# A two-layer decoder trunk in split float32: the high and low weight halves move to other start addresses in SBUF

## The chip, the cores and the metric

The kernel runs on one core of a Trainium2 chip. The metric is the device time of one execution in microseconds (us); lower is better. Before the change the median of 3 runs was 2752.81 us (2752.61 to 2753.01).

## What is computed

Two decoder layers over 256 positions of width 2048, all in float32. Layer 0 mixes tokens with a Mamba-2 block, layer 1 with attention that has a forgetting gate; each layer then has a SwiGLU feed-forward block and a gated per-layer input. Cut to what matters here:

```python
for i in range(2):
    hn = rmsnorm(h, norm_mix_pre[i])
    mix = ssd_mixer(hn, ...) if i == 0 else fox_mixer(hn, ...)   # each: u @ w_in, the mixer, @ w_out
    h = h + rmsnorm(mix, norm_mix_post[i])
    hn = rmsnorm(h, norm_ffn_pre[i])
    ff = (silu(hn @ w_gate[i]) * (hn @ w_up[i])) @ w_down[i]     # 2048 -> 5632 -> 2048
    h = h + rmsnorm(ff, norm_ffn_post[i])
    pe = rmsnorm(p[i] @ ple_w_proj[i], ple_norm[i])
    h = h + sigmoid(h @ ple_w_gate[i]) * pe
```

Nearly all of the work is products of a 256-row activation with large weight matrices, some 500 MB of weights, each used once.

## The kernel before, in words

**Split products.** A float32 product is made of three products in the faster `float32r` type. An activation `x` is held as a high half (rounded) and a low half (the rest), side by side in one tile of 2 x 256 columns; a weight tile `raw` becomes a high half `wh` and a low half `wl` in the same way. The product is `wh*xh + wh*xl + wl*xh`; the term `wl*xl` is left out.

**Stages.** The weights come in 1020 stages of at most 1024 columns on 128 partitions (`emit_stage`, L160). For each, SyncE's queue issues the DMA of `raw` (L170), ScalarE rounds it to `wh` (L182), VectorE subtracts to make `wl` (L187). There are 6 buffers of `raw` and 4 each of `wh` and `wl`.

**Matmuls.** `unit` (L202) takes the stages in order. In the common form a block of 128 x 128 weights is the stationary operand and the activation is the moving one. Each block of `wh` is loaded and 512 columns (high and low activation halves) are streamed past it; then the block of `wl` at the same place is loaded and the 256 columns of the high half are streamed:

```python
PE.matmul(accs[t], lhsT=wh[:, c, t * P:(t + 1) * P],
          rhs=x.rearrange("p a n -> p (a n)"), start=st, stop=False)      # L249
last = PE.matmul(accs[t][:, :T], lhsT=wl[:, c, t * P:(t + 1) * P],
          rhs=x[:, 0, :], start=False, stop=sp)                            # L251
```

So while L249 streams its 512 columns, the weights of the following L251 are loaded, and while L251 streams its 256 columns the `wh` block of the next pair is loaded. This text calls an L249 with its L251 a pair, and the time from the start of one matmul to the start of the next a slot. The last units before a norm use a separate form (L244, L245, L246): three matmuls of 256 columns, `wh` twice, then `wl`. A third form (L238 to L240, in layer 1's value projection) has the weights as the moving operand, 412 or 416 columns wide. The products of the per-layer input (L436, L439, L440) are again three of 256 columns, with the activation tile `psp`.

**The activations** lie in several pools: `x` tiles in `xp` (the most used: normed input of the mixers and of the feed-forward block), `xq` (half of the Mamba block's output), `a` in `act0` and `act1` (the feed-forward block's hidden activations), `xb` (the input of layer 1's mixer), and `psp` at the far end.

**Where tiles lie in SBUF** is set by pools that are laid one behind another in the order in which they are opened: `cp`, `wp` (raw, wh, wl), `hp` (the residual stream `h`), `xp`, `ev` (temporaries), `gap`, and then the pools that come and go (`xq`, `xb`, `act0`, ...). Two pads of 96 bytes are there already: 24 spare columns behind the last tile of `hp` (L376), which push `xp` along, and the tile of 24 columns in `gap` (L381), which pushes all behind it. Every step inside `wh`, `wl` and the activation tiles that a matmul of the pair or of the separate form makes is a multiple of 512 bytes, so each kind of tile has one start address modulo 256 bytes for all its blocks.

The order of the instructions on each engine comes from a scheduler that does not look at addresses.

Of the kernel before, what the change touches and what calls it, by code (L numbers as in the profile page):

```python
# [7 lines left out]
F32 = mybir.dt.float32  # L8
F32R = mybir.dt.float32r
# [5 lines left out]
P = 128  # L15
# [12 lines left out]
SW = 1024  # L28
# [3 lines left out]
WB = 4  # L32
# [7 lines left out]
HELD = 6  # L40
WARM = 10
TAIL_WIDE = 2

_VEC = {}
_NV = 0
# [11 lines left out]
def tile_trunk(ctx, tc, a, out):  # L57
    nc = tc.nc
    mult, add, sub, mx_, mn_ = ALU.mult, ALU.add, ALU.subtract, ALU.max, ALU.min
    V, A, G, PE = nc.vector, nc.scalar, nc.gpsimd, nc.tensor  # L60

    def pool(stack, name, bufs=1, **kw):
        return stack.enter_context(tc.tile_pool(name=name, bufs=bufs, **kw))

    cp = pool(ctx, "cp")
    wp = pool(ctx, "wp")
    hp = pool(ctx, "hp")
    xp = pool(ctx, "xp", bufs=16)
    ev = pool(ctx, "ev", bufs=2)
    gap = pool(ctx, "gap")  # L70
# [5 lines left out]
    def nm(s):  # L76
        cnt[0] += 1
        return f"{s}_{cnt[0]}"
# [78 lines left out]
    def after(ins):  # L157
        return nullcontext() if ins is None else tc.issue_after(ins.ins)

    def emit_stage(a_ins=None, v_ins=None):  # L160
        i = len(emitted)
        cols, r, kc, n = stages[i]

        def view(t):
            return t[:, :kc * n].rearrange("p (c n) -> p c n", n=n)

        raw = wp.tile([P, SW], F32, tag="raw", name=f"raw{i}", bufs=RAWB)
        o = 0
        for W, c0, w in cols:
            nc.sync.dma_start(  # L170
                out=view(raw)[:, :, o:o + w],
                in_=W[r:r + kc * P, c0:c0 + w].rearrange("(c p) n -> p c n", p=P))
            o += w
        wh = wp.tile([P, SW], F32R, tag="wh", name=f"wh{i}", bufs=WB)
        wl = wp.tile([P, SW], F32R, tag="wl", name=f"wl{i}", bufs=WB)
        if a_ins is None:
            a_ins, turn_a[0] = turn_a[0], None
        with ExitStack() as order:
            for ins in [a_ins] + lag[0]:
                order.enter_context(after(ins))  # L180
            lag[:] = [lag[1], []]
            low_a[0] = A.copy(out=wh[:, :kc * n], in_=raw[:, :kc * n])  # L182
        with ExitStack() as order:
            for ins in [v_ins] + turn:
                order.enter_context(after(ins))
            turn.clear()
            low[0] = V.tensor_tensor(out=wl[:, :kc * n], in0=raw[:, :kc * n],  # L187
                                     in1=wh.bitcast(F32)[:, :kc * n], op=sub)
        emitted.append((view(wh), view(wl), kc))

    def next_stage(look=LOOK):
        i = taken[0]
        taken[0] += 1
        while len(emitted) < len(stages) and len(emitted) <= i + look:
            emit_stage()
        return emitted[i]
# [5 lines left out]
    def unit(rhs, evac, tok=False, pre=None, pops=1, late=(), merge=1, look=LOOK, sep=False):  # L202
# [4 lines left out]
        if nt == 6:  # L207
            merge = TAIL_WIDE
        accs = [psa.tile([P, 512], F32, tag="acc", name=nm("acc")) for _ in range(nt)]
# [168 lines left out]
    warm = cp.tile([P, 2], F32, name="warm")  # L378
    V.memset(ones, 1.0)
    V.memset(mhalf, -0.5)  # L380
    G.memset(gap.tile([P, 24], F32, name="gap0"), 0.0)  # L381
    A.activation(warm, mhalf, AF.Exp)

    def load_x(c):
# [6 lines left out]
    for c in range(3):  # L391
        emit_stage(None, None if c else lo0)
        load_x(c + 1)
# [55 lines left out]
    def post_norm(fill):  # L449
        for f in fill[:FILL_A]:  # L450
            f()
        rs = rstd_small(ssb, D)
        for _ in range(PRE_A):
            emit_stage(mark[0], dmark[0])
        for f in fill[FILL_A:FILL_B]:
            f()
        ps = rstd_wide(rs, None)
        for f in fill[FILL_B:]:
            f()
        return ps  # L460
# [976 lines left out]
```

## Time and profile before

| | |
|---|---|
| median of 3 runs | 2752.81 us |
| span of the profiled execution | 2751.0 us, 1.8 us under that median |
| TensorE (PE) busy | 2743.8 us, 100% |
| VectorE (DVE) busy | 1906.4 us, 69% |
| ScalarE (ACT) busy | 1479.8 us, 54% |
| GpSimd (POOL) busy | 48.5 us, 2% |
| DMA | 519.58 MB, mean 189 GB/s |

How to read it: PE is the row of the matmuls and PEld that of the weight loads that go on beside them. Matmuls are pipelined: one starts before the one ahead of it has left, and the end shown is modelled, so neither the busy share nor the mean duration says how fast they follow each other. That is read from the start times of the timeline. A group's row gives busy time, then the mean length of one, then the idle time of the engine just before its instructions and what ended it.

### The profile page before, as it was taken

How to read it: one execution, taken by the hardware profiler on the slowest of the kernel's cores; microseconds unless marked ns; L12 is line 12 of the kernel's file. 1: busy time of each engine (PE TensorE's matmuls, PEld its weight loads, DVE VectorE, ACT ScalarE, POOL GpSimd, SP SyncE). 2: the span in 40 equal slices, each digit the busy share in tenths (PEclk: the TensorE clock that was granted, in tenths of full speed). 3: DMA queues.
4: the chain of work that ended last, by engine and by line, in shares of the span. 5: the costliest groups of instructions: out<-in, count | busy, mean ns of one | idle time of the engine just before them, and what ended most of it. 6: DMA issues, size and time to landing. Idle time of an engine off the chain costs nothing.

```text
span 2751.0 us, 43135 instructions
## 1 busy us (share of the span) xinstructions
PE 2743.8 (100%) x16342; PEld 2434.7 (89%) x16342; DVE 1906.4 (69%) x3147; ACT 1479.8 (54%) x2455; POOL 48.5 (2%) x104
## 2 busy tenths in 40 slices
PE   9999999999999999999999999999999999999999
PEld 8888888889888888888898998889888888888898
DVE  8888888754976545666568656766876545666577
ACT  6577677554654444445456544555654444445454
POOL 0000000000000000000000000000000000000000
PEclk9999999999999999999999999999999999999999
DMA  7666666565666556666556676555666556656554
GB/s 262 187 200 192 188 193 188 163 210 166 191 201 189 190 191 189 188 175 200 195 161 196 186 221 181 177 162 163 195 206 189 187 192 188 194 169 201 198 163 167
DMA packets 262656, 519.58 MB, mean 189 GB/s; under 512 B 17408, under 2 KB 44192, under 8 KB 262448
## 3 DMA queue, kind: packets, MB, share of 16 engines
q1 hardware_dynamic: 258784, 504.54, 59.6%
q0 software_dynamic: 3520, 12.15, 1.4%
q8 instruction: 128, 2.10, 0.3%
q14 instruction: 80, 0.66, 0.1%
q10 hardware_dynamic: 144, 0.14, 0.0%
HBM read 514.58 MB, written 2.18 MB: 188 GB/s over the span
## 4 chain that ended last, share of the span: by engine, by line
PE 99%; DVE 1%; ACT 0%; issue 0%; DMA 0%; DVEq 0%; ACTq 0%
PE acc L249 58%; PE acc L251 30%; PE acc L245 1%; PE acc L246 1%; PE acc L244 1%; PE acc L238 1%; PE acc L239 1%; PE acc L240 1%; PE mi L1004 1%; PE mi L1269 0%; PE mi L1317 0%; PE mi L347 0%; PE mi L963 0%; PE acc L436 0%; PE mi L331 0%
## 5 line engine op out<-in xcount | busy, mean ns | idle before, releaser
L249 PE MATMUL acc<-x,wh 128*128 128x512 f32 x4992 | 1696.7, 393 | 0.9 <-DVE x L389 0.5
L187 DVE TENSOR_TENSOR wl<-raw,wh 128x1024 fp32r<-128x1024 f32 (+4 forms) x1020 | 1169.3, 1152 | 725.1 <-ACT wh L182 723.5
L182 ACT CAST wh<-raw 128x1024 fp32r<-128x1024 f32 (+4 forms) x1020 | 1004.2, 991 | 968.2 <-PE acc L249 841.1
L251 PE MATMUL acc<-x,wl 128*128 128x256 f32 x4992 | 1317.0, 280 | 0.1
L249 PEld LDWEIGHTS acc<-x,wh 128*128 128x128 f32 x4992 | 922.4, 188 | 189.6 <-issue 1.3
L251 PEld LDWEIGHTS acc<-x,wl 128*128 128x128 f32 x4992 | 923.6, 188 | 25.6 <-issue 2.4
L249 PE MATMUL acc<-a,wh 128*128 128x512 f32 x1232 | 425.5, 391 | 0.0
L251 PE MATMUL acc<-a,wl 128*128 128x256 f32 x1232 | 341.9, 282 | 0.0
L249 PEld LDWEIGHTS acc<-a,wh 128*128 128x128 f32 x1232 | 229.9, 188 | 47.1
L251 PEld LDWEIGHTS acc<-a,wl 128*128 128x128 f32 x1232 | 232.6, 189 | 2.2
L249 PE MATMUL acc<-xb,wh 128*128 128x512 f32 x512 | 179.4, 393 | 0.0
L277 ACT COPY tb<-acc 128x256 f32<-128x256 f32 x400 | 140.1, 369 | 49.1 <-PE acc L251 25.0
L251 PE MATMUL acc<-xb,wl 128*128 128x256 f32 x512 | 144.9, 284 | 0.0
L249 PEld LDWEIGHTS acc<-xb,wh 128*128 128x128 f32 x512 | 95.6, 188 | 19.5
L251 PEld LDWEIGHTS acc<-xb,wl 128*128 128x128 f32 x512 | 96.7, 189 | 0.8 <-issue 0.2
L249 PE MATMUL acc<-xq,wh 128*128 128x512 f32 x224 | 77.7, 390 | 0.0
L900 DVE SCALAR_TENSOR_TENSOR g<-xr,vec,g 128x256 f32<-128x256 f32 x144 | 63.4, 478 | 10.8 <-ACT g L897 10.6
L278 DVE TENSOR_TENSOR g<-acc,tb 128x256 f32<-128x256 f32 x171 | 65.1, 417 | 0.4
L251 PE MATMUL acc<-xq,wl 128*128 128x256 f32 x224 | 63.0, 282 | 0.0
L984 ACT ACTIVATE E<-ab,bias 128x128 f32<-128x128 f32 x192 | 59.9, 392 | 1.2 <-DMA ab<-acd 1.2
L301 DVE TENSOR_TENSOR ssb<-ssb,sq 128x256 f32<-128x256 f32 x120 | 50.5, 421 | 12.3 <-ACT sq L300 8.9
L337 POOL TENSOR_TENSOR rs<-ms,mhalf 128x2 f32<-128x2 f32 x18 | 22.6, 1253 | 1993.1 <-DVE ms L334 1993.1
(228 smaller groups left out, 2156.9 us busy)
## 6 DMA issues: line engine op xcount, KB each, us to landing
raw<-down SPq DMA_DIRECT2D x176, 512.0 KB, 4.1
raw<-ssd_in SPq DMA_DIRECT2D x144, 512.0 KB, 4.5
raw<-gate SPq DMA_DIRECT2D x128, 512.0 KB, 4.3
raw<-up SPq DMA_DIRECT2D x128, 512.0 KB, 4.4
raw<-fox_in SPq DMA_DIRECT2D x64, 512.0 KB, 4.2
raw<-gate SPq DMA_DIRECT2D x64, 384.0 KB, 3.3
raw<-up SPq DMA_DIRECT2D x64, 384.0 KB, 3.6
raw<-ssd_out SPq DMA_DIRECT2D x40, 512.0 KB, 3.8
```

Source lines behind the costliest of these rows:

```text
L182: low_a[0] = A.copy(out=wh[:, :kc * n], in_=raw[:, :kc * n])
L187: low[0] = V.tensor_tensor(out=wl[:, :kc * n], in0=raw[:, :kc * n], in1=wh.bitcast(F32)[:, :kc * n], op=sub)
L238: PE.matmul(o, lhsT=xh, rhs=wh[:, c, :], start=st, stop=False)
L239: PE.matmul(o, lhsT=xh, rhs=wl[:, c, :], start=False, stop=False)
L240: last = PE.matmul(o, lhsT=x[:, 1, t * P:(t + 1) * P], rhs=wh[:, c, :], start=False, stop=sp)
L249: PE.matmul(accs[t], lhsT=wh[:, c, t * P:(t + 1) * P], rhs=x.rearrange("p a n -> p (a n)"), start=st, stop=False)
L251: last = PE.matmul(accs[t][:, :T], lhsT=wl[:, c, t * P:(t + 1) * P], rhs=x[:, 0, :], start=False, stop=sp)
L277: i = A.copy(out=tb[:np_], in_=acc[:np_, T:2 * T])
L278: took[0] = (i, V.tensor_tensor(out=o, in0=acc[:np_, :T], in1=tb[:np_], op=add))
L301: last_v[0] = V.tensor_tensor(out=acc, in0=acc, in1=sq, op=add)
L900: V.scalar_tensor_tensor(out=c, in0=xr[:, k:k + T], scalar=col(f"conv_w{k}", cc), in1=c, op0=mult, op1=add)
L984: A.activation(E[:, i, b * P:(b + 1) * P], ab[:, i, lo:lo + P], AF.Relu, scale=-1.0, bias=bias3[:, b, h0 + i:h0 + i + 1])
```

## The change

The tiles `wh` and `wl` leave the pool `wp` and get pools of their own, with a pad of 64 bytes between them. The pool of `x` gets a pad of 96 bytes ahead of it, and the pad ahead of the come-and-go pools grows from 96 to 224 bytes. Sizes, counts of buffers and all arithmetic stay as they are.

```diff
+GAP_L = 16
+GAP_X = 24
+GAP_A = 56
...
     wp = pool(ctx, "wp")
+    whp = pool(ctx, "whp")
+    gap_l = pool(ctx, "gap_l")
+    wlp = pool(ctx, "wlp")
     hp = pool(ctx, "hp")
+    gap_x = pool(ctx, "gap_x")
     xp = pool(ctx, "xp", bufs=16)
...
-        wh = wp.tile([P, SW], F32R, tag="wh", name=f"wh{i}", bufs=WB)
-        wl = wp.tile([P, SW], F32R, tag="wl", name=f"wl{i}", bufs=WB)
+        wh = whp.tile([P, SW], F32R, tag="wh", name=f"wh{i}", bufs=WB)
+        wl = wlp.tile([P, SW], F32R, tag="wl", name=f"wl{i}", bufs=WB)
...
-    G.memset(gap.tile([P, 24], F32, name="gap0"), 0.0)
+    for g_, n_ in ((gap_l, GAP_L), (gap_x, GAP_X), (gap, GAP_A)):
+        G.memset(g_.tile([P, n_], F32, name=nm("gap")), 0.0)
```

What it does to the addresses, from the built programs (byte address of the first tile in a partition, and in brackets that address modulo 256):

| tile | before | after |
|---|---|---|
| `raw` | 19488 (32) | 19488 (32) |
| `wh` | 44064 (32) | 44064 (32) |
| `wl` | 60448 (32) | 60512 (96) |
| `h` | 76832 (32) | 76896 (96) |
| `x` | 93376 (192) | 93536 (96) |
| `xq`, `xb`, `a` | 137792 (64) | 138080 (96) |
| `psp` | 225248 (224) | 225248 (224) |

The distance from the moving activation to the weights that are loaded beside it, modulo 256 bytes, follows from it:

| activation | to `wh` before | to `wl` before | to `wh` after | to `wl` after |
|---|---|---|---|---|
| `x` | 96 | 96 | 192 | 0 |
| `xq`, `xb`, `a` | 224 | 224 | 192 | 0 |
| `psp` | 64 | 64 | 64 | 128 |

The instructions of PE, DVE, ACT and SP stand in the same order in both programs. The one engine whose list differs is GpSimd's, at the program's start. Before:

```order
5 L1433 UNCONDITIONAL_BRANCH
6 L381 MEMSET gap_103 128x24
7 L893 MEMSET xr_617 128x3
8 L893 MEMSET xr_631 128x3
9 L337 ISA
```

And after, at the same place:

```order
5 L1441 UNCONDITIONAL_BRANCH
6 L389 MEMSET gap_115 128x16
7 L389 MEMSET gap_117 128x24
8 L389 MEMSET gap_119 128x56
9 L901 MEMSET xr_633 128x3
10 L901 MEMSET xr_647 128x3
11 L344 ISA
```

One fill of a pad has become three; nothing else moved.

## The prediction

> **What bounds the kernel now.** I read the page first (its span, the busy row, the clock row, the chain that ended last), then the groups of instructions by shape, then the timeline at a few places. From the page:
>
> ```profile
> span 2751.0 us, 43135 instructions
> PE 2743.8 (100%) x16342; PEld 2434.7 (89%) x16342; DVE 1906.4 (69%) x3147; ACT 1479.8 (54%) x2455; POOL 48.5 (2%) x104
> PEclk9999999999999999999999999999999999999999
> PE 99%; DVE 1%; ACT 0%; issue 0%; DMA 0%; DVEq 0%; ACTq 0%
> ```
>
> The chain of waits is TensorE nearly from end to end, at the full granted clock. So only what makes its matmuls follow each other faster or slower moves the end. The groups tell how many there are:
>
> ```profile
> L249 PE MATMUL acc<-x,wh 128*128 128x512 f32 x4992 | 1696.7, 393 | 0.9 <-DVE x L389 0.5 <-DVE gz L278 0.2
> L249 PE MATMUL acc<-a,wh 128*128 128x512 f32 x1232 | 425.5, 391 | 0.0
> L249 PE MATMUL acc<-xb,wh 128*128 128x512 f32 x512 | 179.4, 393 | 0.0
> L249 PE MATMUL acc<-xq,wh 128*128 128x512 f32 x224 | 77.7, 390 | 0.0
> L244 PE MATMUL acc<-a,wh 128*128 128x256 f32 x176 | 49.0, 279 | 0.0
> L244 PE MATMUL acc<-x,wh 128*128 128x256 f32 x128 | 35.7, 280 | 0.0
> L244 PE MATMUL acc<-xq,wh 128*128 128x256 f32 x32 | 8.9, 279 | 0.0
> L239 PE MATMUL acc<-wl,xb 128*128 128x412 f32 x128 | 44.7, 350 | 0.0
> ```
>
> That is 4992 + 1232 + 512 + 224 = 6960 pairs of L249 and L251, and 336 triples of L244 to L246, 1008 matmuls of 256 columns. Idle time is nil, so a stall, if there is one, sits inside the slots. The mean lengths (393, 391) overlap and don't help; the start times do. First the `x` pairs (activation 96 bytes before the weights), then the `a` pairs (224 bytes), each with the first and the last row of a steady stretch:
>
> ```profile
> 2083.11 0.39 PE L249 MATMUL acc<-x,wh 128*128 128x512 f32 x1
> ...
> 2092.12 0.39 PE L249 MATMUL acc<-x,wh 128*128 128x512 f32 x1
> ```
>
> ```profile
> 1002.04 0.39 PE L249 MATMUL acc<-a,wh 128*128 128x512 f32 x1
> 1002.27 0.28 PE L251 MATMUL acc<-a,wl 128*128 128x256 f32 x1
> ...
> 1011.75 0.39 PE L249 MATMUL acc<-a,wh 128*128 128x512 f32 x1
> ```
>
> 26 pairs in 9.01 us are 346.5 ns a pair, 28 in 9.71 us are 346.8: the same at both distances. Over these rows L249's slot is 229 ns on the mean and L251's 118. So the pairs take 6960 x 346.7 ns = 2413 us, 88% of the span, and a change of 1 ns in a pair is 7 us.
>
> Does a slot depend on addresses at all? Matmuls of one shape, 256 columns past 128 x 128 weights, show it. Separate form, `x` (distance 96) in one place and in another, then `a` (224), then the per-layer products with `psp` (64) at two places:
>
> ```profile
> 659.95 0.28 PE L244 MATMUL acc<-x,wh 128*128 128x256 f32 x1
> ...
> 661.03 0.28 PE L244 MATMUL acc<-x,wh 128*128 128x256 f32 x1
> ```
>
> ```profile
> 1511.33 0.28 PE L244 MATMUL acc<-x,wh 128*128 128x256 f32 x1
> ...
> 1512.03 0.28 PE L244 MATMUL acc<-x,wh 128*128 128x256 f32 x1
> ```
>
> ```profile
> 1399.96 0.28 PE L244 MATMUL acc<-a,wh 128*128 128x256 f32 x1
> ...
> 1401.01 0.28 PE L244 MATMUL acc<-a,wh 128*128 128x256 f32 x1
> ```
>
> ```profile
> 683.29 0.28 PE L440 MATMUL acc<-psp,wl 128*128 128x256 f32 x1
> ...
> 684.35 0.28 PE L440 MATMUL acc<-psp,wl 128*128 128x256 f32 x1
> ...
> 686.24 0.28 PE L440 MATMUL acc<-psp,wl 128*128 128x256 f32 x1
> ...
> 686.92 0.28 PE L440 MATMUL acc<-psp,wl 128*128 128x256 f32 x1
> ```
>
> 9 slots in 1.08 us are 120 ns; 6 in 0.70 are 116.7; 9 in 1.05 are 116.7; 9 in 1.06 are 117.8; 6 in 0.68 are 113.3. So one shape has slots from 113 to 120 ns, nobody waits for data, and a stretch keeps its rate: once in step, the two reads (activation and next weights) stay in step. Two rates occur at one distance too (120 and 116.7 at 96; 117.8 and 113.3 at 64), so the distance selects among rates and does not fix one.
>
> **The change part by part.** *Addresses of the pair form.* It removes no instruction from TensorE and adds none. L249 now loads `wl` at distance 0, L251 loads `wh` at 192, for all 6960 pairs. No row of before has either distance. For the 118 ns slot of L251 the bounds are the 256-column rows: 113.3 below, 120 above. Distance 192 lies half a cycle from 64, and the two distances that the pairs have now, half a cycle apart as well, give one rate; so the `psp` rows at 64 are the nearest. They show 113.3 and 117.8; I take their middle, 115.5, a gain of 2.5 ns. For the 229 ns slot of L249 the lower bound is twice the fastest 256 columns, 226.7; the upper bound comes from the first unit, where five L249 follow each other and then five L251:
>
> ```profile
> 19.67 1.33 PE L249 MATMUL acc<-x,wh 128*128 128x512 f32 x5
> 20.83 0.75 PE L251 MATMUL acc<-x,wl 128*128 128x256 f32 x5
> 21.42 1.33 PE L249 MATMUL acc<-x,wh 128*128 128x512 f32 x5
> ```
>
> Five in 1.16 us are 232 ns; the five L251 take 0.59 us, 118 each. L249 is thus within 2.3 ns of its lower bound and I take no change for it. Together: 6960 x -2.5 ns = -17.4 us, with bounds of 6960 x (-2.3 - 4.7) = -49 us and 6960 x (3 + 2) = +35 us.
>
> *The separate form.* Two of three slots load `wh` (192), one loads `wl` (0): 672 x (115.5 - 117) ns = -1.0 us; bounds 1008 x (113.3 - 117) = -4 and 1008 x (120 - 117) = +3 us.
>
> *The value projection* (L238 to L240, 480 matmuls) has the roles exchanged and other distances; at 3 ns either way, the spread between rates of the rows above, it is 1.4 us, taken as 0.
>
> *Pads.* Two more fills on GpSimd:
>
> ```profile
> 0.74 0.12 POOL L381 MEMSET gap<- 128x24 f32 x1 [0.29 <-POOLq L1428]
> 0.79 0.13 POOL L893 MEMSET xr<- 128x3 f32 x2
> ```
>
> 0.05 us from one fill to the next, at 0.7 us, on an engine that is 2% busy; the next thing on its list is needed by a convolution that comes far later. Nothing.
>
> *What covers the other engines.* ScalarE, VectorE and the DMA write and read at shifted addresses too. A slower conversion would be hidden as long as VectorE keeps its slack, least in the first 480 us:
>
> ```profile
> 0.00:480.00 480.00, 478.47 (x2895) 413.90 (x2896) 412.58 (x735) 333.75 (x640) 23.10 (x77) 1.00 0.64 202
> L187 DVE TENSOR_TENSOR wl<-raw,wh 128x1024 fp32r<-128x1024 f32 (+4 forms) x1020 | 1169.3, 1152 | 725.1 <-ACT wh L182 723.5
> ```
>
> VectorE is busy 412.58 of 480 us there (the fourth of the columns: PE, PEld, DVE after the length), so a TensorE that needs 1% less, 475 us, still finds its weights. If L187 took 10% longer, that would be 117 us against 725 us of idle time ahead of it. Taken as 0.
>
> Sum against the profiled execution: 2751.0 - 17.4 - 1.0 = 2732.6 us; the median of the runs lies 1.8 us over that span, so **2734 us**.
>
> **The rivals.** *No change.* The reads don't meet, or the streams fall into the old step again: then the pair stays at 346.7 ns and the time at 2753 us. For it speaks that distances 96 and 224 give the same pair to 0.3 ns; against it, that one shape runs at 113 and at 120 ns. The Trainium skill (TensorE: Matmul & The Clock Gate, Part 2, the step on LDWEIGHTS) says the same as this rival: TensorE has two independent read ports, so that loading the next weights takes nothing from the running matmul. By that rule alone the change is worth 0; the spread of slots does not agree with it.
>
> *Slower: a level start.* The load and the matmul beside it begin together:
>
> ```profile
> 2083.11 0.39 PE L249 MATMUL acc<-x,wh 128*128 128x512 f32 x1
> 2083.11 0.19 PEld L251 LDWEIGHTS acc<-x,wl 128*128 128x128 f32 x1
> ```
>
> At distance 0 both reads then start at the same place of the 256-byte cycle, in every one of 6960 pairs. If that collides, L249 goes to the 232 ns of the first unit and L251, pushed out of step, to 120: 352 ns, +5.3 x 6960 = +37 us, with +3 for the separate form: 2793 us. It decides from a pair of 347.5 ns on. Against it: a collision at the start only could also be the one that puts the streams out of each other's way for the rest.
>
> *Both slots gain.* If L249 goes to 226.7 and all slots of 256 columns to 113.3, the pair is 340 ns: -46.6 us and -4 us, 2702 us. Rows show the second half of this, none the first. A sentence apart: the same page of the Trainium skill (Back-to-back issue gap) has columns / 2.4 + 2.5 ns, an estimate of 216 + 109 = 325 ns for a pair and by that of about 2600 us if every excess were the placement's; no row comes near it.
>
> **How the numbers follow.** Forecast (L251 gains 1 to 4.7 ns, L249 holds): 0.42, 2718 to 2746 us. Both gain: 0.15. No change: 0.15. Slower: 0.28, since nothing shown excludes the level start. The median of a few runs tells about 0.2% (5.5 us, 0.8 ns a pair) from no change. So faster 0.57, same 0.15, slower 0.28. The range takes in the forecast, no change, and the prices of the other two: 2696 to 2794 us; beyond lie a stronger form of either, some 0.15 together.
>
> **What would show it.** Right: start to start, L249 stays at 228 to 230 ns and L251 falls to 113 to 117, alike for `x`, `a`, `xq`, `xb`; L244 to L246 follow. Wrong: L249 at 232 or more (level start), a pair at 346 to 347 (no change), or L249 below 226 (it was not at its bound). A gain in slots that isn't in the span would show as idle time ahead of L249, released by VectorE or ScalarE.

## The result, and the profile after

The changed kernel takes 2720.88 us (median of 4 runs, 2719.67 to 2721.03) against 2752.82 us before: a ratio of 0.9882 (95% interval 0.9868 to 0.9896), 32 us faster. From the page of the changed kernel:

```profile
span 2719.0 us, 43137 instructions
PE 2711.1 (100%) x16342; PEld 2410.5 (89%) x16342; DVE 1905.3 (70%) x3147; ACT 1480.7 (54%) x2455; POOL 48.8 (2%) x106
PEclk9999999999999999999999999999999999999999
PE 97%; DVE 1%; ACT 1%; issue 1%; DMA 0%; DVEq 0%; ACTq 0%
L194 DVE TENSOR_TENSOR wl<-raw,wh 128x1024 fp32r<-128x1024 f32 (+4 forms) x1020 | 1169.4, 1152 | 694.0 <-ACT wh L189 688.9
```

TensorE's busy time fell by 32.7 us with the same count of matmuls at the same clock; VectorE's subtraction (now L194) takes what it took, 1152 ns, and only the idle time ahead of it shrank, from 725.1 to 694.0 us. So what changed is the rate of the matmuls, and little else. The timeline of the changed kernel in the steady `x` stretch, first and last row (L256 is the old L249, L258 the old L251):

```profile
2099.76 0.39 PE L256 MATMUL acc<-x,wh 128*128 128x512 f32 x1
2099.99 0.28 PE L258 MATMUL acc<-x,wl 128*128 128x256 f32 x1
...
2108.94 0.39 PE L256 MATMUL acc<-x,wh 128*128 128x512 f32 x1
```

27 pairs in 9.18 us are 340.0 ns, against 346.5 before. That is the rate of the rival "both slots gain": over all pairs of the trace at 339 to 341 ns the two slots are 226.7 and 113.3 on the mean. But it is not the rate everywhere. At 348 us, four small matmuls of a norm come between the pairs:

```profile
348.33 0.50 PE L338 MATMUL mi<-ones,gss 128*128 128x1 f32 x4
...
349.12 0.40 PE L256 MATMUL acc<-x,wh 128*128 128x512 f32 x1
...
353.32 0.40 PE L256 MATMUL acc<-x,wh 128*128 128x512 f32 x1
353.56 0.22 PE L354 MATMUL mi<-identr,rh 128*128 128x128 f32 x1
...
354.46 0.39 PE L256 MATMUL acc<-x,wh 128*128 128x512 f32 x1
354.80 0.39 PE L256 MATMUL acc<-x,wh 128*128 128x512 f32 x1
...
356.84 0.39 PE L256 MATMUL acc<-x,wh 128*128 128x512 f32 x1
```

Behind them 12 pairs take 4.20 us, 350 ns each, without a wait; then other small matmuls come (L354), and behind those 7 pairs take 2.38 us, 340 ns each. Same tiles, same placement, two rates, and the change from one to the other at an interruption. This text calls such a rate a lock. Where 16 or more pairs follow each other without another matmul or a stall between them (98 stretches before, 97 after, up to 118 pairs long), none changes its rate behind its fifth pair; in the run with the distances (64, 0) further down, three of 100 do.

Added up over the whole trace from start to start (stalls, slots over 245, 130 or 200 ns, apart):

| form | count | before, mean slot | after, mean slot | us |
|---|---|---|---|---|
| 512 columns, `wh` | 6920 | 229.61 | 227.70 | -13.2 |
| 256 columns, `wl` | 6910 | 117.70 | 114.37 | -23.0 |
| separate form | 1007 | 117.18 | 117.79 | +0.6 |
| value projection | 478 | 187.29 | 189.16 | +0.9 |
| per-layer products | 184 | 116.1 | 118.4 | +0.4 |
| stalls inside these | | 10.7 us | 13.3 us | +2.6 |

The sum, -31.7 us, is the difference of the spans, 2751.0 - 2719.0, but for 0.3. Of the 5991 pairs that stand directly between two other matmuls of the pair form, 90.3% took 345 to 348 ns before; after, 85.3% take 339 to 341, 7.3% 349 to 352 and 3.7% still 345 to 348.

### The profile page after: what moved, and what is told of

It reads as the page before. It is cut to its first block, busy times and chain, and to the rows that moved or that the text cites. A ratio compares the mean times of both kernels' runs of the same rounds, so it can differ in the third digit from the quotient of the medians.

```text
span 2719.0 us, 43137 instructions
## 1 busy us (share of the span) xinstructions
PE 2711.1 (100%) x16342; PEld 2410.5 (89%) x16342; DVE 1905.3 (70%) x3147; ACT 1480.7 (54%) x2455; POOL 48.8 (2%) x106
## 4 chain that ended last, share of the span: by engine, by line
PE 97%; DVE 1%; ACT 1%; issue 1%; DMA 0%; DVEq 0%; ACTq 0%
PE acc L256 56%; PE acc L258 29%; PE acc L253 1%; PE acc L252 1%; PE acc L251 1%; PE acc L247 1%; PE acc L246 1%; PE acc L245 1%; PE mi L1012 1%; DVE wl L194 1%; ACT E L992 1%; PE mi L1277 0%; PE mi L1325 0%; ACT wh L189 0%; PE acc L444 0%
## 5 line engine op out<-in xcount | busy, mean ns | idle before, releaser
L256 PE MATMUL acc<-x,wh 128*128 128x512 f32 x4992 | 1673.4, 391 | 0.9 <-DVE gz L285 0.8
L194 DVE TENSOR_TENSOR wl<-raw,wh 128x1024 fp32r<-128x1024 f32 (+4 forms) x1020 | 1169.4, 1152 | 694.0 <-ACT wh L189 688.9
L258 PE MATMUL acc<-x,wl 128*128 128x256 f32 x4992 | 1305.2, 278 | 0.9 <-DVE wl L194 0.7
L256 PEld LDWEIGHTS acc<-x,wh 128*128 128x128 f32 x4992 | 921.8, 188 | 181.8 <-issue 1.3
L258 PEld LDWEIGHTS acc<-x,wl 128*128 128x128 f32 x4992 | 923.0, 188 | 26.4 <-DVE wl L194 3.4
L256 PE MATMUL acc<-a,wh 128*128 128x512 f32 x1232 | 417.5, 389 | 0.0
L258 PE MATMUL acc<-a,wl 128*128 128x256 f32 x1232 | 335.2, 276 | 0.0
L256 PEld LDWEIGHTS acc<-a,wh 128*128 128x128 f32 x1232 | 229.8, 188 | 46.2
L258 PEld LDWEIGHTS acc<-a,wl 128*128 128x128 f32 x1232 | 231.3, 188 | 2.1
L256 PE MATMUL acc<-xb,wh 128*128 128x512 f32 x512 | 176.6, 392 | 0.0
L258 PE MATMUL acc<-xb,wl 128*128 128x256 f32 x512 | 142.4, 279 | 0.0
L256 PEld LDWEIGHTS acc<-xb,wh 128*128 128x128 f32 x512 | 95.6, 188 | 19.2
L258 PEld LDWEIGHTS acc<-xb,wl 128*128 128x128 f32 x512 | 96.2, 188 | 0.8 <-issue 0.2
L256 PE MATMUL acc<-xq,wh 128*128 128x512 f32 x224 | 76.3, 389 | 0.0
L258 PE MATMUL acc<-xq,wl 128*128 128x256 f32 x224 | 61.7, 276 | 0.0
```

The lines of the kernel that those rows point to most:

```text
L256: PE.matmul(accs[t], lhsT=wh[:, c, t * P:(t + 1) * P], rhs=x.rearrange("p a n -> p (a n)"), start=st, stop=False)
```

## The experiments

**Theory 1** is the prediction's: each slot follows the distance of the weights that are loaded in it, L249's that of `wl`, L251's that of `wh`. **Theory 2**: activation stream and weight loads fall in step over a whole pair; a placement (both distances together) only offers locks, and what goes ahead picks one. In the runs at (96, 0), (192, 96), (64, 128) and (64, 0) only the pad sizes differ from the changed kernel, and an empty pad is not filled; distances are given as (`wh`, `wl`), so before is (96, 96) and (224, 224), after (192, 0).

### One distance at a time

`wl` level, `wh` as before, (96, 0):

```diff
-GAP_L = 16
+GAP_L = 40
```

> Weights' distances from the activation: wh 96 as before the change, wl 0 as after it. Theory 1 (each slot follows the distance of the weights loaded in it): the 512-column slot falls from 229 to 227 ns, the 256-column slot stays at 118; 6960 x -1.9 ns = -13 us, 2740 us. Theory 2 (the two loads of a pair lock together, and half of the change is not half of the gain): the pair stays near 347 ns, 2750 to 2756 us, or goes to a third rate that neither kernel shows.

`wh` as after, `wl` as before, (192, 96):

```diff
-GAP_L = 16
-GAP_X = 24
+GAP_L = 40
+GAP_X = 0
```

> Distances: wh 192 as after the change, wl 96 as before it. Theory 1: the 256-column slot falls from 118 to 114.4 ns, the 512-column slot stays at 229 to 230; 6960 x -3.3 ns = -23 us, 2730 us. Theory 2: the pair stays near 347 ns or goes to a rate of its own; 2750 us or more.

The first took 2757.09 us, a ratio of 1.0015 (1.0005 to 1.0024) to before; the second 2764.87 us, 1.0043 (1.0026 to 1.0060). Timeline of the first, then of the second, in a steady `x` stretch:

```profile
2059.85 0.39 PE L256 MATMUL acc<-x,wh 128*128 128x512 f32 x1
...
2068.86 0.39 PE L256 MATMUL acc<-x,wh 128*128 128x512 f32 x1
```

```profile
2069.71 0.40 PE L256 MATMUL acc<-x,wh 128*128 128x512 f32 x1
...
2074.94 0.40 PE L256 MATMUL acc<-x,wh 128*128 128x512 f32 x1
```

26 pairs in 9.01 us, 346.5 ns; 15 in 5.23, 348.7 ns. With `wl` level alone the 512-column slot did not fall to 227, it rose (mean 231.16) while the 256-column slot fell (116.53); with `wh` at 192 alone the 256-column slot stayed at 117.08, and the 512-column slot rose to 231.86. Either half by itself loses, 4 and 12 us, together they gain 32 us. Theory 1 falls. (The first time lies 1 us over the range that theory 2 had been given.)

### Is the cycle 128 bytes or 256?

Both distances moved by 128, (64, 128):

```diff
-GAP_X = 24
+GAP_X = 56
```

> Both distances of the changed kernel shifted by half a cycle: wh 64, wl 128. If the cycle that matters is 128 bytes, as the equal pairs at 96 and 224 before the change let one think, this is the changed kernel again: pair 340 ns, 2721 us within 5. If the cycle is 256 bytes, the pair is another one, anywhere from 340 to 352 ns, 2720 to 2795 us; more than 5 us away from 2721 decides for 256.

It took 2784.96 us, 1.0116 (1.0101 to 1.0131). Timeline:

```profile
2059.71 0.39 PE L256 MATMUL acc<-x,wh 128*128 128x512 f32 x1
...
2068.90 0.39 PE L256 MATMUL acc<-x,wh 128*128 128x512 f32 x1
```

26 pairs in 9.19 us are 353.5 ns, over the 352 that had been allowed, and a lock that neither kernel showed as its steady rate; 77% of the pairs run at 353 to 357. The half cycle of the prediction's nearest-row argument is refuted: 128 bytes make 64 us here. That 256 bytes are a whole cycle is shown for `wl` by the run of the separate form's edit, further down: its `wl` tiles are 4352 bytes long, so neighbouring buffers lie 17 x 256 bytes apart, and 84.7% of its pairs run at 339 to 341 all the same.

### A map of the placements

The changed kernel with a block of extra matmuls ahead of the first unit. They use a tile `mb` of activation values and write a PSUM tile that is not read; the column at which the weights start sets the distance:

```diff
...
+        def mm_(n, o_, m=P):
+            ins = PE.matmul(wps[:m, :n], lhsT=mb[:, o_:o_ + m], rhs=xf[:, :n], start=True, stop=True)
+            tc.keep_in_program_order(ins)
+        for rep, first in ((0, 64), (1, 144)):
+            for dh in range(8):
+                for dl in range(8):
+                    mm_(first, 960)
+                    for _ in range(14):
+                        mm_(512, 8 * dh)
+                        mm_(256, 512 + 8 * dl)
...
```

> The changed kernel with a block of extra matmuls near its start, on data of no use: for each of the 64 combinations of the two distances in steps of 32 bytes, twice with another matmul ahead, 14 pairs of 512 and 256 columns; then 512-column and 256-column matmuls whose loads are 32, 64 or 128 columns wide, at each distance. Its result is read from the slots, its time is some 700 us longer. Theory 1: the 512-column slot depends on wl's distance alone and the 256-column slot on wh's alone (spread over the other distance under 1 ns). Theory 2: at least 4 ns of spread over the other distance. Both: at (96, 96) and (224, 224) 346.7 ns a pair, at (192, 0) 340. On the floor: if 226.7 and 113.3 ns are the activation stream's own pace, 32-column loads do not get under them by more than 1 ns; if they still hold a cost of loading, 32-column loads fall towards 216 and 109 ns.

An entry is one run of 14 pairs with the matmul ahead of it. The mean pair in ns, worked out from the starts of the fifth to the thirteenth pair of each entry, for the entry behind 144 columns (rows: `wh` at 0 to 224 bytes, columns: `wl` at 0 to 224):

```
       0     32     64     96    128    160    192    224
  0  346.7  347.4  346.6  346.7  346.7  351.1  350.4  352.7
 32  350.4  352.4  348.6  350.0  353.9  349.9  351.1  347.0
 64  340.0  351.1  353.3  353.6  349.3  353.3  353.3  351.1
 96  346.7  351.8  348.1  346.7  350.2  351.9  348.9  350.0
128  351.3  353.3  346.7  351.9  351.1  351.1  346.7  346.7
160  349.1  346.7  348.9  353.9  346.7  350.1  352.4  346.7
192  340.0  348.3  353.3  348.9  346.7  349.9  348.9  348.9
224  353.3  348.9  346.4  346.7  348.9  353.3  353.3  346.7
```

Both placements of before stand at 346.7, that of after at 340.0, and 340.0 is reached at two of the 64, never with either distance by itself: `wl` at 0 gives anything from 340 to 353, `wh` at 192 from 340 to 353. With 64 columns ahead instead of 144, (192, 0) gave 350.0 and (64, 0) 353.7, while (96, 96) and (224, 224) gave 346.7 again. That is theory 2.

The map also answers a rival that the two kernels leave open, that the new addresses only keep the writes of VectorE, ScalarE and the DMA out of TensorE's way. While the map runs, no other engine works. After the length the columns are PE, PEld, DVE, ACT and POOL, then the clock, the DMA share and its GB/s:

```profile
100.00:700.00 600.00, 600.00 (x3491) 516.70 (x3491) 0.00 (x0) 0.00 (x0) 0.00 (x0) 1.00 0.00 1
```

The rates of both kernels, 346.7 and 340.0, are there all the same, so they come from TensorE's own loads and streams.

Loads of 32 columns, a quarter as wide, in streams of one width throughout did not get under the lowest slots: 230.4 to 238.5 ns behind 512 columns, 113.2 to 117.8 behind 256; with loads of 128 columns the same streams gave 229.2 to 233.9 and 115.1 to 120.0.

### The second good place, and the same place elsewhere

(64, 0), and the changed kernel's (192, 0) with `wh`, `wl` and the activations of the pairs all moved by 64 bytes:

```diff
-GAP_L = 16
+GAP_L = 48
```

> Distances wh 64, wl 0: the only other combination that reached 340 ns a pair in the map, once of two entries. Theory 2 (joint lock, one cycle of 256 bytes, several locks to one placement): most pairs at 340, the rest at the map's other rate, 353.7; with the same share of fast pairs as the changed kernel 2721 us, with fewer more: 2715 to 2745. Theory 1 (each slot by its own distance) has no reason for it: wh at 64 with wl at 128 ran 355 ns a pair, so it gives 2750 us or more.

```diff
+    gap_w = pool(ctx, "gap_w")
     whp = pool(ctx, "whp")
...
-    for g_, n_ in ((gap_l, GAP_L), (gap_x, GAP_X), (gap, GAP_A)):
+    for g_, n_ in ((gap_w, 16), (gap_l, GAP_L), (gap_x, GAP_X), (gap, GAP_A)):
```

> The changed kernel with weights and activations all moved by 64 bytes, the distances kept (wh 192, wl 0). If distances decide: 2721 us within 4, 340 ns for some 85% of the alternating pairs. Rival (it is the place of the activation or of the low halves in the 256-byte cycle that decides, 96 for both in the changed kernel): the pair leaves 340, 2735 us or more.

(64, 0) took 2760.01 us, 1.0025 (1.0016 to 1.0035): a miss for the size that was expected. 24% of its pairs run at 339 to 341 and 48% at 349 to 352, not at the 353.7 of the map. (The 355 ns of the expectation for (64, 128) are the 353.5 read above.) Its timeline in one of the latter stretches, 26 pairs in 9.10 us, 350.0 ns:

```profile
2059.80 0.39 PE L256 MATMUL acc<-x,wh 128*128 128x512 f32 x1
...
2068.90 0.39 PE L256 MATMUL acc<-x,wh 128*128 128x512 f32 x1
```

The moved kernel took 2720.58 us, 0.9882 (0.9865 to 0.9898), the changed kernel again, with 84.9% of the pairs at 339 to 341. Timeline, 26 pairs in 8.85 us, 340.4 ns:

```profile
2099.94 0.39 PE L257 MATMUL acc<-x,wh 128*128 128x512 f32 x1
...
2108.79 0.39 PE L257 MATMUL acc<-x,wh 128*128 128x512 f32 x1
```

So it is the distances that count, not the place of a tile in the cycle, as far as one shift can show it.

### What the entry does

The same kind of block, with 16 entries to a placement, and then the separate form at the 64 placements:

```diff
+        for dh, dl in ((48, 0), (16, 0), (24, 24), (56, 56), (44, 0), (52, 0), (48, 4), (48, 60)):
+            for first in range(64, 320, 16):
+                mm_(first, 960)
+                for _ in range(14):
+                    mm_(512, dh)
+                    mm_(256, 512 + dl)
...
+                for _ in range(10):
+                    mm_(256, 8 * dh)
+                    mm_(256, 8 * dh)
+                    mm_(256, 512 + 8 * dl)
```

> The changed kernel with a block of extra matmuls near its start: eight combinations of the distances, each entered 16 times behind a matmul of 64 to 304 columns, 14 pairs each; then 10 rounds of the separate form (256 columns, wh, wh, wl) at the 64 combinations. If a placement only offers locks and the entry picks one: at (192, 0) and (64, 0) part of the 16 entries end at 340 and part at 350 or 354, while (96, 96) and (224, 224) end at 346.7 from all. If the rate is a property of the placement alone, all 16 entries of a combination end alike within 1 ns. For the separate form: if its mean can go under 116 ns a slot somewhere, it has a better placement than (192, 0), which gives 117.8 in the changed kernel.

Entries by the rate at which they end:

```
(192, 0)    11 at 340.0, 5 at 350.0
(64, 0)      7 at 340.0, 6 at 350.0, 3 at 353.3
(96, 96)    16 at 346.7
(224, 224)  16 at 346.7
(192, 16)   13 at 340.0, 3 at 353.4
```

The other three, (176, 0), (208, 0) and (192, 240), ended between 346.7 and 353.5, none at 340. The placements of before have one lock in all these entries, that of after has two, and the entry picks. But the number of columns of the matmul ahead does not pick alone: behind 64 columns (192, 0) ended at 350.0 in the first map and at 340.0 in this one, behind 144 columns it was the other way round. In the separate form 62 of the 64 placements lie between 115.6 and 124.4 ns a slot; (192, 64) and (64, 192) give 113.3.

A third map, wh at 184 to 200 and wl at 0 to 28 in steps of 4 bytes, 10 entries each:

```diff
+        for dh in (46, 47, 48, 49, 50):
+            for dl in range(8):
+                for first in range(64, 304, 24):
...
```

> The changed kernel with a block of extra matmuls near its start: wh at 184 to 200 bytes and wl at 0 to 28 bytes past the activation in steps of 4, each of the 40 combinations entered 10 times behind a matmul of 64 to 280 columns, 12 pairs each. The coarse maps gave 340 ns from 11 of 16 entries at (192, 0) and from 13 of 16 at (192, 16). If the lock at 340 has a middle, some combination between or beside them ends at 340 from all 10 entries; if the share is an accident of each placement, none does, and the shares scatter between 0 and 9 of 10. Nowhere should a pair run under 339.5 ns, if 340 is the activation stream's own pace (768 columns at 0.443 ns).

Of its 400 entries none settled under 340.0 ns. 340 was met only with `wh` at 192 exactly: 8 of 10 entries at `wl` 0, 9 of 10 at 16, 4 of 10 at 12 (two of the four only from the seventh pair on). A shift of 4 bytes of either half from (192, 0) already gives 347 to 350 on the mean. The lock is narrow and no placement has it from every entry.

### Two ways to go on from it

The maps point to `wl` at 16 bytes, and to 64 bytes for the stages of the separate form. Both need spare columns in the tile of `wl`, paid for with 1 KB of GpSimd's DMA scratch:

```diff
-SCRATCH = 8192
+SCRATCH = 7168
...
+        lo = 4
-        wl = wlp.tile([P, SW], F32R, tag="wl", name=f"wl{i}", bufs=WB)
+        wl = wlp.tile([P, SW + 64], F32R, tag="wl", name=f"wl{i}", bufs=WB)[:, lo:lo + SW]
```

> The changed kernel with the low halves 16 bytes past the activation instead of level (wh still 192), for all stages; the tile of the low halves gets 64 spare columns for it and GpSimd's DMA scratch 1 KB less. By the fine maps 22 of 26 entries end at 340 ns against 19 of 26 at 0, and the others at 353.4 instead of 350. If that share carries over to the kernel: 2714 to 2721 us. If the kernel's entries after a wait are not like the map's: anything up to 2735, with the share of pairs at 339 to 341 lower than the changed kernel's 85%.

For the separate form `lo = 16 if i in sep_stages else 0`, where `sep_stages` are the stages of the units that run it:

> The changed kernel with the low halves 64 bytes past the activation in the stages of the separate form alone (wh 192 there), level elsewhere; same spare columns and scratch. The map gave 113.3 ns a slot for the separate form at (192, 64) against 117.8 at (192, 0): 1008 x -4.5 ns = -4.5 us, 2716 us. If the form has other locks that the map's single entry did not show: 117 to 120 ns, 2720 to 2724.

And both, `lo = 16 if i in sep_stages else 4`:

> Both edits together: 64 bytes in the separate form's stages, 16 elsewhere. If the two act on different matmuls the gains or losses of the two runs add, within 1.5 us; by the maps 2710 to 2717 us, faster than both kernels of this case.

`wl` at 16 took 2775.68 us, 1.0082 (1.0067 to 1.0097), a clear miss: 20.3% of the pairs at 339 to 341, 71.7% at 353 to 357. Its timeline, 14 pairs in 4.95 us, 353.6 ns:

```profile
2059.84 0.40 PE L257 MATMUL acc<-x,wh 128*128 128x512 f32 x1
...
2064.79 0.40 PE L257 MATMUL acc<-x,wh 128*128 128x512 f32 x1
```

The map named its two locks and had their shares the wrong way round: the kernel's interruptions are not the map's entries. The spare columns and the smaller scratch are not the reason, since the next run has both.

The separate form's edit alone took 2715.86 us (2715.52 to 2716.66), a ratio to before of 0.9866 (0.9849 to 0.9882): the fastest here, 5.0 us under the changed kernel, whose runs (2719.67 to 2721.03) lie apart from it. The separate form in the changed kernel, then with the edit, from the timeline:

```profile
656.82 0.28 PE L251 MATMUL acc<-x,wh 128*128 128x256 f32 x1
...
658.94 0.28 PE L251 MATMUL acc<-x,wh 128*128 128x256 f32 x1
```

```profile
1379.90 0.28 PE L256 MATMUL acc<-a,wh 128*128 128x256 f32 x1
...
1389.76 0.28 PE L256 MATMUL acc<-a,wh 128*128 128x256 f32 x1
```

18 slots in 2.12 us, 117.8 ns; 87 in 9.86 us, 113.3 ns. The sum over the form fell from 118.6 to 114.1 us, 4.5 of the 5.0 us.

Both edits together took 2773.16 us, 1.0073 (1.0058 to 1.0089): another miss, and the two effects do not add within 1.5 us as was expected. The time is 2.5 us over their sum, and the separate form alone makes these 2.5 us: its mean slot is 115.8 ns here against 113.35 with its own edit alone, at the same distances. The distances alone do not fix its rate either.

## Why the prediction was right, and where its steps were not

The direction and the range held; the forecast of 18.8 us is 59% of the 32 that came. The time even lies in the forecast's own branch, 2718 to 2746 us, but not by the branch's mechanism, "L251 gains, L249 holds". Of its sign of being right a part came: L251 fell to 114.4 ns on the mean, and 340 ns became the commonest pair of `x`, `a`, `xq` and `xb` alike; but L249 went to 227.7 (228 to 230 was named), and L244 to L246 did not follow. That the change gains at all was luck as far as the prediction's argument goes: (192, 96) gives L251 the same distance and lost 12 us, and (64, 0) gives it the one that the argument took as equal and lost 7.

- *TensorE's slots are all that matters, and nothing else is late next.* Right but for 2.6 us, by which the stalls grew. VectorE's work in the first 480 us grew by 1.9 us and still fits, but for two waits of L258 for its `wl`, 0.7 us in total and 0.5 the longest, that the list of waits of before does not have:

```profile
PE acc L258 <- DVE wl L194: 0.7, 2, 0.5
```

```profile
0.00:480.00 480.00, 478.08 (x2918) 414.44 (x2919) 414.52 (x742) 334.38 (x641) 23.31 (x79) 1.00 0.64 202
```

- *A stretch keeps its rate; the distance selects among rates and does not fix one.* Right, and the maps show it directly, for the two distances together. (Of its rows, the 116.7 ns at 1511 us are 117.5 by the unrounded starts; that leaves two rates at one distance.)
- *L251's slot, -2.5 ns for 17.4 us.* Mis-sized: -3.3 ns, 23.0 us. The reason given for its value, that 192 lies half a cycle from 64 and is therefore like it, is wrong: the pair half a cycle away runs at 353.5 ns.
- *L249's slot, no change.* Wrong, -1.9 ns and 13.2 us. The step that failed is the bookkeeping by single slots: the pair is what locks, and the lock at 340 has both slots at their fastest. Its lower bound, twice the fastest 256-column stretch, is the 226.7 ns of the lock, and the bound for the pair, 226.7 + 113.3 = 340.0, is the lowest steady rate of any placement tried. So the rival "both slots gain" had the mechanism nearer than the forecast, though its price, 2702 us, is 19 us under the time: 10 us for the pairs that are not at 340, 5 for the separate form, which the rival had at 113.3 and which went to 117.8, and 4 for stalls, value projection and per-layer products.
- *The separate form, -1.0 us, the value projection 0.* Measured +0.6 and +0.9. The per-layer products, whose distance to `wl` went from 64 to 128 and which the sum leaves out, took 0.4 us more.
- *No change.* Not so. The Trainium skill (TensorE: Matmul & The Clock Gate, Part 2, the step on LDWEIGHTS) has it that a load takes no read bandwidth from the running matmul. The runs do not agree that a load is without effect: with the same matmuls and loads, placements alone made 2720.58, 2757.09, 2764.87 and 2784.96 us. That it is bandwidth which the load takes is not shown. The formula of the same page of the Trainium skill (Back-to-back issue gap; there for a matmul by itself; 325 ns a pair as an estimate) was not reached either; the shortest steady pair is 340.0 ns.
- *The level start.* `wl` at distance 0 gave 340 to 353 ns depending on `wh`, so starting level neither costs nor gains by itself.

What stays open: how a load and a stream hold each other up, what picks the lock at an interruption, and what sets 340 ns. That 32-column loads run no faster fits a pace of the activation stream itself, but no run had a stream without loads.

## What to carry to other kernels

When matmuls follow each other without a wait, read their slots from start to start: two rates of one shape at full clock, each constant over a stretch, were here the sign that start addresses could change the rate. Tune the two distances (activation to the weights loaded under it) as one pair of numbers, since here each half alone lost and both together won. A block of spare matmuls in one run maps which rates a placement offers, but the share in which the kernel takes them has to be timed in the kernel.

## What the runs showed of the hardware that was not expected

- The rate of float32r pairs (512 and 256 columns on 128 x 128 weights) depends on the distances modulo 256 bytes, down to 4: 340.0 ns at (192, 0), 347 to 350 with either half moved by 4 bytes, 353.5 at (64, 128). Moving weights and activations together by 64 bytes changes nothing (2720.58 against 2720.88 us).
- One placement can hold two or three locks (340.0, 350.0, 353.3 at (64, 0)); the entry picks, and not by the width of the last matmul alone: behind 64 columns (192, 0) ran at 350.0 in one map and at 340.0 in another. Once reached, within a few pairs, a lock mostly holds to the next interruption.
- The floor of what was seen in these two shapes is 0.443 ns a column, 113.3 ns for 256 and 226.7 for 512, with loads of 128 columns and no shorter with loads of 32.
